# Row factors of the first norm moved onto results, with transposed input and three tiles side by side, and the convolutions of the up-projection emitted last

## Chip, core and metric

The kernel runs on one core of a Trainium2 chip. The metric is the device time of one execution in microseconds (us). The core has a matrix engine (TensorE, PE in the profile; PEld is its weight load), a vector engine (VectorE, DVE), a scalar engine for activations (ScalarE, ACT), GpSimd (POOL), and 16 DMA engines, which this kernel feeds from one queue, that of SyncE (SP).

## The reference

A hybrid decoder block for one sequence of 1024 positions and 1024 channels, in float32:

```
def rms_norm(x, w):
    y = x * rsqrt(mean(x * x, axis=-1) + EPS)
    return y * w

h = rms_norm(x, norm_mix_w)
proj = h @ w_in            # one product for all that follows:
q_nsa, kv_nsa, g_nsa, q_ret, k_ret, v_ret, g_ret, g_merge = split(proj)
y_a = nsa_attention(rope(q_nsa), kv_nsa, sigmoid(g_nsa)) @ w_nsa_branch
y_b = (group_norm(retention(q_ret, k_ret, v_ret)) * silu(g_ret)) @ w_ret_branch
x = x + (sigmoid(g_a) * y_a + sigmoid(g_b) * y_b) @ w_mix_out    # g_a, g_b from g_merge
h = rms_norm(x, norm_ffn_w)
u = causal_dwconv(h @ w_ffn_up)      # width 3, with a bias
x = x + (silu(u_gate) * u_val) @ w_ffn_down
return rms_norm(x, norm_final_w)
```

The factor 1/rms belongs to a row of x. It can be applied to the row before the product with w_in, or to the same row of the product's result.

## The kernel before

Rows are cut into NT = 8 tiles of 128 positions, channels into KT = 8 tiles of 128. Every float32 operand of a matrix product is split into a high part, a copy to the format fp32r on ACT, and a low part, the remainder, a subtraction on DVE (`split`, L174); `mm3` (L278) then does three products for each step: high by high, high by low, low by high.

First norm (L319 to L334): for each tile the rows are fetched into a buffer of the pool `big` (eight buffers), `normed` takes squares on ACT, the root, a few one-column steps on DVE and one scaling by rstd and gain, and `transposed_split` (L269) transposes the eight 128x128 blocks on PE and splits them into `hh` and `hl`, which hold h transposed. The weights of the first projection (`kvw`) are fetched in four pairs of channel tiles, two at t = 0 and two at t = 1, through two raw buffers (`wr`, pool `wraw`).

Projections: `proj` (L341) runs over the row tiles, 24 products of 512 columns each, and calls an evacuation for each tile. The first projection gives the keys and values of two branches (`evac_kv`), the next the third branch and the branch gates (`evac_kw`, 280 columns), then the queries (`evac_q`). The attention follows, with the products of the merge gates filled in between; their results are stored in DRAM transposed (`gate_d`). Then comes the retention (`evac_qk`, `values`, `evac_g`), and the merge: `gated` (L976) loads one merge gate of 128x1024 and takes its sigmoid; gates from the second eight use three buffers `gb`, which also serve sums of w_ffn_down (`t_sums`).

Up-projection (L1237 to L1299): 22 column tiles f, computed by a Strassen-like scheme with seven products of 12 matrix instructions each for one f. `first_weights` and `other_weights` fetch and split the weights of one f, with sums on DVE. The first five f have two of their seven products done earlier (`begun`). `up(f, w)` does the rest: each product is followed by a sum on DVE, and at the end two `conv` (one ACT step and two scalar_tensor_tensor steps on DVE each), a Silu, one multiplication and a store.

Tiles come from pools, and an instruction waits where its buffer is still in use. Where no order is written out by hand, each engine's instructions are ordered ahead of time, the one earlier in the program first where several are ready; each engine then runs its list in that order. In the stretches marked `manual_schedule` the order is that of the program (attention: that of a planner, `Plan`).

Of the kernel before, what the change touches and what calls it, by code (L numbers as in the profile page):

```python
# [10 lines left out]
F32 = mybir.dt.float32  # L11
# [7 lines left out]
P = 128  # L19
D = 1024  # L20
# [143 lines left out]
def hybrid_block(ctx: ExitStack, tc: tile.TileContext, a, c, out):  # L164
# [153 lines left out]

    with tc.tile_pool(name="n1", bufs=2, side="right") as n1:  # L319
        gain = n1.tile([P, D], F32, name="gain1", bufs=1)  # L320
        for t in range(NT):
            xt = big.tile([P, D], F32, name="big")
            n = 2 if t == 0 else 1
            for i in range(0, D, D // n):
                nc.sync.dma_start(xt[:, i:i + D // n], a["x"][0, t * P:(t + 1) * P, i:i + D // n])
            if t == 0:
                nc.sync.dma_start(gain, bcast_rows(a["norm_mix_w"][0], D))
                nc.sync.dma_start(ident, c["ident"])
            h = big.tile([P, D], F32, name="big")
            normed(n1, xt, gain, h, n)  # L330
            transposed_split(psA, h, hh, hl, t)
            if t < 2:
                kvw.more()
                kvw.more()  # L334
# [6 lines left out]
    def proj(w, n, evac, tag="mm", pool=None, other=iter(()), cuts=(0, KT), keep=0, pairs=False):  # L341


        last = NT - 2 if pairs else NT
        for t in range(NT):
            if t <= last:
                ps = [(pool or psA).tile([P, 512], F32, name=tag) for _ in range(2 if t == last else 1)]
                for k0, k1 in zip(range(0, KT, 2), range(2, KT + 1, 2)) if t == last else zip(cuts, cuts[1:]):
                    for i, x in enumerate(ps):
# [5 lines left out]
            evac(t, ps[0] if t <= last else ps[1])  # L355
# [38 lines left out]
    def v_store(b, t, ps):  # L394
        split(vhl[b][:, t, :, 0:DH], vhl[b][:, t, :, DH:], ps)
# [6 lines left out]
    def evac_kv(t, ps):  # L402
        nc.scalar.activation(kvc[:, t].rearrange("p a g d -> p (a g d)"), ps[:, 0:256], AF.Copy)
# [100 lines left out]
    def evac_q(t, ps):  # L504
        nc.scalar.activation(qsb[:, t].rearrange("p h d -> p (h d)"), ps, AF.Copy, scale=DH ** -0.5)
        rope16(qsb[:, t], t, H, np_)
# [296 lines left out]
    nc.sync.dma_start(rope, c["rope128"])  # L803
    dmask = rp.tile([P, RH, P], F32, name="dmask")
# [26 lines left out]
    for p in range(2):  # L831
# [48 lines left out]
        def values(t, ps):  # L880
            v = big.tile([P, 2, 2, DV], F32R, name="v", tag="big")
            split(v[:, 0], v[:, 1], ps.rearrange("p (h e) -> p h e", h=2))
# [121 lines left out]
    for ch in range(2):  # L1004
        nx = Weights(w_a, 0, 4, [(512, 512)]) if ch == 0 else Weights(w_b, 0, KT, [(0, 512)])
        for i in range(4):
# [7 lines left out]
            if (ch * 4 + i) % 2 == 0:  # L1014
                x, y = ([q[:, 0:512], q[:, 512:S]] for q in
                        (mp.tile([P, S], F32, name="tq", tag="gb", bufs=3) for _ in range(2)))
                t_sums(t_left.pop(0), x, y)
# [48 lines left out]
    c2p = ups.enter_context(tc.tile_pool(name="c2", bufs=10))  # L1066
# [144 lines left out]
    def other_weights(f):  # L1211
# [13 lines left out]
        hi, lo = (cpool.tile([P, 512], F32R, name=x, bufs=2) for x in ("a22h", "a22l"))  # L1225
# [11 lines left out]
    def up(f, w):  # L1237
# [51 lines left out]
    nx = other_weights(0)  # L1289
    for f in range(FT):  # L1290
# [8 lines left out]
        up(f, w)  # L1299
# [176 lines left out]
_LAYOUT = {"w_ffn_up": _up_layout}  # L1476
# [22 lines left out]
```

## Time and profile before

| | |
|---|---|
| median of 3 runs | 1786.49 us (1784.19 to 1790.05) |
| the profiled execution | 1786.91 us, of which the span of the core is 1785.1 us |
| busy share | PE 98%, DVE 67%, ACT 45%, POOL 7% |
| DMA | 188.32 MB, mean 105 GB/s over the span |

The profile shows one execution. The span runs from the first to the last instruction of the core. A group of instructions is given by line, engine, operation and tiles (out<-in). Products on PE overlap, so the length of one is not the step from one to the next.

### The profile page before, as it was taken

To read this page: it belongs to the slowest core of one execution; us is meant where nothing else is said; L and a number is where in the kernel's file an instruction comes from. 1 tells how busy PE (TensorE), PEld (TensorE's weight loads), DVE (VectorE), ACT (ScalarE), POOL (GpSimd) and SP (SyncE) were. 2 spreads that over 40 slices of the span, in tenths; PEclk is the share of its full clock that TensorE was granted. 3 is DMA by queue.
4 is the path that set the end of the run, shared out by engine and by line. 5 is a ranking of instruction groups with operands and counts; after the bars stand their busy time and mean duration, and the time that the engine had idled before them with its cause. 6 is when DMAs were issued, how large, how long until landed. Compare 5 with 4: busy or idle time off the path is not lost. (4 is left out here: it accounts for less than half of the span.)

```text
span 1785.1 us, 22560 instructions
## 1 busy us (share of the span) xinstructions
PE 1742.7 (98%) x8331; PEld 1430.9 (80%) x8331; DVE 1189.1 (67%) x2343; ACT 803.9 (45%) x1464; POOL 120.6 (7%) x72
## 2 busy tenths in 40 slices
PE   7999999999999999999999999889999999999998
PEld 6987888878788888888888878767888888878886
DVE  7445878787876554456455447877677677678666
ACT  6334666665654244136332215434444444353344
POOL 0000010020100000000000001201211211000000
PEclk9999999999999999999999999999999999999999
DMA  6121011020203101111485483323323323396353
GB/s 230 55 84 54 19 42 48 25 65 25 66 24 101 47 1 54 53 36 48 134 281 188 148 295 101 118 71 112 124 95 118 118 95 107 104 345 217 99 161 112
DMA packets 90155, 188.32 MB, mean 105 GB/s; under 512 B 8813, under 2 KB 18621, under 8 KB 90045
## 3 DMA queue, kind: packets, MB, share of 16 engines
q1 hardware_dynamic: 90044, 186.88, 32.0%
q8 instruction: 65, 1.06, 0.2%
q14 instruction: 46, 0.37, 0.1%
HBM read 147.00 MB, written 39.85 MB: 105 GB/s over the span
## 5 line engine op out<-in xcount | busy, mean ns | idle before, releaser
L283 PE MATMUL mm<-wh,hh 128*128 128x512 f32 (+1 forms) x576 | 224.1, 389 | 0.3 <-ACT hh L175 0.3
L283 PE MATMUL mm<-wh,hl 128*128 128x512 f32 (+1 forms) x576 | 220.0, 382 | 0.0
L283 PE MATMUL mm<-wl,hh 128*128 128x512 f32 (+1 forms) x576 | 219.8, 382 | 0.0
L209 ACT ACTIVATE wh<-wr 128x1024 fp32r<-128x1024 f32 (+1 forms) x72 | 74.6, 1037 | 154.9 <-PE mm L283 76.8
L175 ACT ACTIVATE wh<-wr 128x1024 fp32r<-128x1024 f32 (+1 forms) x87 | 88.3, 1020 | 102.5 <-PE f L283 49.7
L713 DVE TENSOR_TENSOR pl<-pt,ph 128x512 fp32r<-128x512 f32 (+1 forms) x148 | 100.7, 687 | 41.7 <-ACT ph L710 41.2
L283 PEld LDWEIGHTS mm<-wh,hh 128*128 128x128 f32 x576 | 108.8, 189 | 20.4 <-ACT wh L209 0.9
L283 PEld LDWEIGHTS mm<-wh,hl 128*128 128x128 f32 x576 | 108.7, 189 | 20.5 <-DVE hl L176 0.3
L710 ACT ACTIVATE ph<-pt 128x512 fp32r<-128x512 f32 (+1 forms) x148 | 87.7, 595 | 82.7 <-PE pt L706 74.4
L283 PEld LDWEIGHTS mm<-wl,hh 128*128 128x128 f32 x576 | 108.9, 189 | 19.5 <-DVE wl L215 0.5
L283 PE MATMUL f<-wh,sl 128*128 128x512 f32 x300 | 118.0, 395 | 0.8 <-DVE sl L176 0.8
L283 PE MATMUL f<-wh,sh 128*128 128x512 f32 x300 | 118.4, 395 | 0.0
L283 PE MATMUL f<-wl,sh 128*128 128x512 f32 x300 | 118.4, 395 | 0.0
L176 POOL TENSOR_TENSOR wl<-wr,wh 128x1024 fp32r<-128x1024 f32 x22 | 55.4, 2520 | 899.5 <-ACT wh L175 899.5
L283 PE MATMUL f<-bht,wh 128*128 128x512 f32 x264 | 105.2, 399 | 5.3 <-ACT wh L175 5.3
L283 PE MATMUL f<-bh,wh 128*128 128x512 f32 x264 | 104.2, 395 | 6.2 <-ACT c L1188 6.2
L283 PE MATMUL f<-bht,wl 128*128 128x512 f32 x264 | 105.4, 399 | 4.1 <-DVE wl L176 4.1
L215 DVE TENSOR_TENSOR wl<-wr,wh 128x1024 fp32r<-128x1024 f32 (+1 forms) x60 | 71.4, 1193 | 55.8 <-ACT wh L209 55.0
L772 PE MATMUL fill<-hh,wh 128*128 128x512 f32 x256 | 104.5, 408 | 3.1 <-ACT sg L784 2.1
L628 ACT ACTIVATE big<-big,st 128x640 f32<-128x640 f32 (+7 forms) x128 | 93.5, 731 | 28.0 <-DVE st L624 27.3
L283 PE MATMUL f<-blt,wh 128*128 128x512 f32 x264 | 105.1, 398 | 0.0
L283 PE MATMUL f<-bl,wh 128*128 128x512 f32 x264 | 103.6, 392 | 0.0
(286 smaller groups left out, 4135.1 us busy)
## 6 DMA issues: line engine op xcount, KB each, us to landing
wr<-in_w_ffn_up SPq DMA_DIRECT2D x44, 512.0 KB, 3.9
wr<-in_w_in SPq DMA_DIRECT2D x40, 512.0 KB, 3.7
tq<-in_w_ffn_down SPq DMA_DIRECT2D x44, 256.0 KB, 4.5
t<-tq SPq DMA_DIRECT2D x44, 256.0 KB, 2.8
v<-in_w_ffn_up SPq DMA_DIRECT2D x22, 512.0 KB, 4.3
act<-c SPq DMA_DIRECT2D x22, 512.0 KB, 2.8
wr<-t SPq DMA_DIRECT2D x20, 512.0 KB, 3.6
a<-act SPq DMA_DIRECT2D x33, 256.0 KB, 6.0
```

Of the source, the lines that this page charges most:

```text
L175: nc.scalar.activation(hi, src, AF.Copy)
L176: (engine or nc.vector).tensor_tensor(lo, src, f32(hi), OP.subtract)
L209: nc.scalar.activation(hi[:, :, :self.n], self.raw[len(self.hi)], AF.Copy)
L215: self.engine.tensor_tensor(lo[:, :, :self.n], self.raw[j], f32(self.hi[j][:, :, :self.n]), OP.subtract)
L283: nc.tensor.matmul(ps, stat(sp, kt), mov(mp, kt), start=(first and n == 0), stop=(last and n == 3 * nk - 1), skip_group_check=more)
L628: nc.scalar.activation(probs[b][h], probs[b][h], AF.Exp, scale=-1.0, bias=stat["nm", b][:, h:h + 1], accum_out=stat["w", b][:, h:h + 1])
L710: nc.scalar.activation(bx["h"][:rows], bx["pt"][:rows], AF.Copy)
L713: nc.vector.tensor_tensor(bx["l"][:rows], bx["pt"][:rows], f32(bx["h"][:rows]), OP.subtract)
L772: nc.tensor.matmul(fx["ps"], w.at(sp, kt, i * P, P), hT[mp][:, kt, half * 512:half * 512 + 512], start=(n == 0), stop=(n == 3 * KT - 1))
```

## The change

**First norm.** `x` is also given transposed (`x_t`), and the gain as a column per channel tile. For each row tile the transposed block is fetched, multiplied by the gain on DVE and split straight into `hh` and `hl`, without the factor of the row. The rows of x are fetched too, for the mean square; the factors are kept in `rs` and, for the merge, stored in DRAM (`rs_d`). The weight pairs are asked for around the first tile, and the first three tiles of the first projection run side by side (`lead=3`): each weight pair serves the three before the next.

**Row factors on results.** Each evacuation of a projection multiplies by its row's factor: keys and the compressed branch in their ACT copy, values in `scaled_split`, branch gates in a DVE step, queries with the scale folded into `rs_q`, retention queries and keys through the rope table, its gate in the Silu. The merge gates, stored transposed, are multiplied by a broadcast of all factors (`rb`) on DVE before the sigmoid. The buffers `gb` fall from three to two.

**Up-projection.** `finish(f, ...)` holds both convolutions, the Silu, the product and the store; `up(f, ...)` calls it for f - 1 at its very end, and calls `other_weights(f + 1)` after its third product. `c2` falls from ten to nine buffers, `c4` rises from six to seven, and `a22h`, `a22l` fall from two to one each.

```
     with tc.tile_pool(name="n1", bufs=2, side="right") as n1:
-        gain = n1.tile([P, D], F32, name="gain1", bufs=1)
+        gain = n1.tile([P, KT], F32, name="gain1", bufs=1)
+        nc.sync.dma_start(gain, a["norm_mix_w"])
         for t in range(NT):
-            xt = big.tile([P, D], F32, name="big")
+            xt = big.tile([P, KT, P], F32, name="big")
+            src = a["x_t"].rearrange("(k p) s -> p k s", p=P)[:, :, t * P:(t + 1) * P]
             n = 2 if t == 0 else 1
-            for i in range(0, D, D // n):
-                nc.sync.dma_start(xt[:, i:i + D // n], a["x"][0, t * P:(t + 1) * P, i:i + D // n])
+            for k in range(0, KT, KT // n):
+                ks = slice(k, k + KT // n)
+                nc.sync.dma_start(xt[:, ks], src[:, ks])
+                if t == 0 and k == 0:
+                    kvw.fetch()
+                nc.vector.tensor_mul(xt[:, ks], xt[:, ks],
+                                     gain[:, ks, None].to_broadcast([P, KT // n, P]))
+                split(hh[:, ks, t * P:(t + 1) * P], hl[:, ks, t * P:(t + 1) * P], xt[:, ks])
             if t == 0:
-                nc.sync.dma_start(gain, bcast_rows(a["norm_mix_w"][0], D))
+                kvw.high()
+                kvw.low()
+                for _ in range(3):
+                    kvw.more()
                 nc.sync.dma_start(ident, c["ident"])
-            h = big.tile([P, D], F32, name="big")
-            normed(n1, xt, gain, h, n)
-            transposed_split(psA, h, hh, hl, t)
-            if t < 2:
-                kvw.more()
-                kvw.more()
+            x = big.tile([P, D], F32, name="big")
+            nc.sync.dma_start(x, a["x"][0, t * P:(t + 1) * P, :])
+            *_, v = mean_square(n1, [x], [x])
+            nc.vector.tensor_copy(rs[:, t:t + 1], rstd_of(n1, v))
...
+    nc.vector.tensor_scalar(rs_q, rs, DH ** -0.5, None, op0=OP.mult)
+    rs_d = dram.tile([NT, P], F32, name="rs_d")
+    nc.sync.dma_start(rs_d.rearrange("t p -> p t"), rs)
+
+    def scaled_split(hi, lo, src, t):
+        r = rs[:, t:t + 1]
+        nc.scalar.activation(hi, src, AF.Copy, scale=r)
+        nc.vector.scalar_tensor_tensor(lo, src, r, f32(hi), op0=OP.mult, op1=OP.subtract)
...
-        last = NT - 2 if pairs else NT
+        groups = {0: lead, **({NT - 2: 2} if pairs else {})}
+        ready = []
         for t in range(NT):
...
+            if not ready:
+                ready = [(pool or psA).tile([P, 512], F32, name=tag) for _ in range(groups.get(t, 1))]
+                at = range(0, KT + 1, 2) if len(ready) > 1 else cuts
+                for k0, k1 in zip(at, at[1:]):
+                    for i, x in enumerate(ready):
...
-        nc.scalar.activation(ks, ps, AF.Copy)
+        nc.scalar.activation(ks, ps, AF.Copy, scale=rs[:, t:t + 1])
...
-        split(vhl[b][:, t, :, 0:DH], vhl[b][:, t, :, DH:], ps)
+        scaled_split(vhl[b][:, t, :, 0:DH], vhl[b][:, t, :, DH:], ps, t)
...
-    proj(kvw, 512, evac_kv)
+    proj(kvw, 512, evac_kv, lead=3)
...
-        nc.vector.tensor_copy(gates[:, t].rearrange("p h b -> p (h b)"), ps[:, 256:280])
+        nc.vector.tensor_scalar(gates[:, t].rearrange("p h b -> p (h b)"), ps[:, 256:280], rs[:, t:t + 1], None,
+                                op0=OP.mult)
...
+    for i in range(2):
+        nc.vector.tensor_mul(rope[:, i], rope[:, i], rs[:, :, None].to_broadcast([P, NT, DK // 2]))
...
-            nc.scalar.activation(sg, ps, AF.Silu)
+            nc.scalar.activation(sg, ps, AF.Silu, scale=rs[:, t:t + 1])
...
+    rb = mp.tile([P, S], F32, name="rb")
+    nc.sync.dma_start(rb, bcast_rows(rs_d, S))
+
     def gated(j):
-        m = mp.tile([P, S], F32, name=f"ma{j % KT}" if j < KT else "gb", bufs=1 if j < KT else 3)
+        m = mp.tile([P, S], F32, name=f"ma{j % KT}" if j < KT else "gb", bufs=1 if j < KT else 2)
         nc.sync.dma_start(m, gate_d[j])
+        nc.vector.tensor_mul(m, m, rb)
         nc.scalar.activation(m, m, AF.Sigmoid)
         return m
...
-    c2p = ups.enter_context(tc.tile_pool(name="c2", bufs=10))
+    c2p = ups.enter_context(tc.tile_pool(name="c2", bufs=9))
...
-    cpool = ups.enter_context(tc.tile_pool(name="cp", bufs=6, reuse_waits="tile"))
+    cpool = ups.enter_context(tc.tile_pool(name="cp", bufs=1, reuse_waits="tile"))
...
-        return cpool.tile([P, 2, 512], F32, name="c4")
+        return cpool.tile([P, 2, 512], F32, name="c4", bufs=7)
...
-        hi, lo = (cpool.tile([P, 512], F32R, name=x, bufs=2) for x in ("a22h", "a22l"))
+        hi, lo = (cpool.tile([P, 512], F32R, name=x) for x in ("a22h", "a22l"))
...
-    def up(f, w):
+    def finish(f, cg, cv):
+        yg = conv(cg.rearrange("p a b -> p (a b)"), f)
+        nc.scalar.activation(yg, yg, AF.Silu)
+        yv = conv(cv.rearrange("p a b -> p (a b)"), FT + f)
+        nc.vector.tensor_mul(yg, yg, yv)
+        nc.sync.dma_start(act_d[f], yg.rearrange("p (a b) -> p a b", b=512))
+
+    def up(f, w, before):
+
         x, p1 = begun.pop(f, None) or start_up(fw[f])
...
         nc.vector.tensor_add(cv[:, 1], z, u3)
+        nx = other_weights(f + 1) if f + 1 < FT else None
         if f >= LEAD:
...
-        yg = conv(cg.rearrange("p a b -> p (a b)"), f)
-        nc.scalar.activation(yg, yg, AF.Silu)
-        yv = conv(cv.rearrange("p a b -> p (a b)"), FT + f)
-        nc.vector.tensor_mul(yg, yg, yv)
-        yg = yg.rearrange("p (a b) -> p a b", b=512)
-        nc.sync.dma_start(act_d[f], yg)
+        if before:
+            finish(*before)
+        return (f, cg, cv), nx
...
     for f in range(FT):
-        w, nx = nx, None
-        if f + 1 < FT:
-            if f + 1 >= LEAD:
-                fw[f + 1] = first_weights(f + 1)
-            nx = other_weights(f + 1)
+        if f + 1 < FT and f + 1 >= LEAD:
+            fw[f + 1] = first_weights(f + 1)
...
-        up(f, w)
+        left, nx = up(f, nx, left)
+    finish(*left)
```

## Rows read from the trace of the kernel before

**Rows 1.** The page's first part: busy time, share of span, instructions of each engine.
```profile
PE 1742.7 (98%) x8331; PEld 1430.9 (80%) x8331; DVE 1189.1 (67%) x2343; ACT 803.9 (45%) x1464; POOL 120.6 (7%) x72
```
**Rows 2.** Windows: length, busy of PE, PEld, DVE, ACT, POOL; PEclk, DMA share, GB/s.
```profile
0.00:66.80 66.80, 57.68 (x271) 45.61 (x271) 38.32 (x117) 34.19 (x85) 2.86 (x9) 1.00 0.48 158
600.00:700.00 100.00, 99.94 (x534) 85.72 (x533) 55.23 (x134) 47.17 (x89) 0.00 (x0) 1.00 0.15 43
930.00:1010.00 80.00, 80.00 (x355) 66.24 (x354) 42.17 (x40) 20.90 (x20) 0.00 (x0) 1.00 0.48 164
1100.00:1147.00 47.00, 40.75 (x184) 32.60 (x183) 44.02 (x64) 27.05 (x51) 14.68 (x6) 0.96 0.32 104
1147.00:1245.00 98.00, 88.60 (x362) 69.49 (x361) 71.09 (x82) 37.40 (x40) 11.22 (x7) 0.97 0.27 91
1245.00:1560.00 315.00, 315.00 (x1368) 256.37 (x1367) 229.93 (x263) 134.14 (x147) 55.91 (x30) 1.00 0.33 109
1560.00:1785.10 225.10, 217.24 (x935) 175.65 (x933) 157.19 (x203) 96.67 (x132) 0.00 (x0) 0.99 0.56 187
2.00:11.00 9.00, 1.97 (x8) 1.57 (x8) 2.65 (x8) 3.37 (x10) 0.00 (x0) 1.00 0.93 306
```
**Rows 3.** Waits of PE: line, waited for; us in total, times, longest.
```profile
PE tp L275 <- DVE big L267: 8.8, 1, 8.8
PE f L283 <- ACT c L1188: 6.2, 4, 3.2
PE f L283 <- ACT wh L175: 5.3, 3, 2.2
PE f L283 <- DVE wl L176: 4.1, 4, 1.2
```
**Rows 4.** Timeline of the first stage: start, length, engine, line, operation, idle before.
```profile
0.74 0.87 SPq L325 DMA_DIRECT2D big<-in_x  x2
3.39 0.63 ACT L256 ACTIVATE big<-big 128x512 f32<-128x512 f32 x1 [1.16 <-DMA big<-in_x]
8.78 1.97 PE L275 MATMUL tp<-ident,big 128*128 128x128 f32 x8 [8.78 <-DVE big L267]
11.09 0.79 PE L283 MATMUL mm<-wh,hh 128*128 128x512 f32 x1 [0.34 <-ACT hh L175]
...
16.05 0.63 PE L283 MATMUL mm<-wl,hh 128*128 128x512 f32 x1
...
66.80 0.37 PE L283 MATMUL mm<-wh,hh 128*128 128x280 f32 x1
```
**Rows 5.** Timeline of PE: transposes between products, and 18 steps of products.
```profile
37.40 0.39 PE L283 MATMUL mm<-wl,hh 128*128 128x512 f32 x1
37.76 1.06 PE L275 MATMUL tp<-ident,big 128*128 128x128 f32 x8
38.58 0.47 PE L283 MATMUL mm<-wh,hl 128*128 128x512 f32 x1
...
45.19 0.39 PE L283 MATMUL mm<-wh,hl 128*128 128x512 f32 x1
...
49.29 0.39 PE L283 MATMUL mm<-wh,hl 128*128 128x512 f32 x1
```
**Rows 6.** DMA, 35 to 40 us: queue, packets, MB, share of 16 engines.
```profile
q1 hardware_dynamic: 1550, 1.54, 93.1%
```
**Rows 7.** Timeline around one stall of PE in the up-projection.
```profile
1184.93 2.47 DVE L1233 SCALAR_TENSOR_TENSOR c<-c,cw,c 128x1023 f32<-128x1023 f32 x2
...
1189.70 0.69 DVE L1218 TENSOR_TENSOR c<-c,wr 128x512 f32<-128x512 f32 x1
1190.42 1.06 ACT L175 ACTIVATE wh<-c 128x1024 fp32r<-128x1024 f32 x1 [0.68 <-DVE c L1218]
1191.53 0.50 PE L283 MATMUL f<-bht,wh 128*128 128x512 f32 x1 [2.24 <-ACT wh L175]
1192.04 1.22 DVE L176 TENSOR_TENSOR wl<-c,wh 128x1024 fp32r<-128x1024 f32 x1
```

More of the change, by code (lines that the diff above doesn't have):

```diff
@@ L317, in hybrid_block @@
     kvw = Weights(w_in, 0, KT, [(C_KV, 512)], late=True)
+    rs = const.tile([P, NT], F32, name="rs")
     with tc.tile_pool(name="n1", bufs=2, side="right") as n1:
-        gain = n1.tile([P, D], F32, name="gain1", bufs=1)
+        gain = n1.tile([P, KT], F32, name="gain1", bufs=1)
+        nc.sync.dma_start(gain, a["norm_mix_w"])
         for t in range(NT):
-            xt = big.tile([P, D], F32, name="big")
+            xt = big.tile([P, KT, P], F32, name="big")
+            src = a["x_t"].rearrange("(k p) s -> p k s", p=P)[:, :, t * P:(t + 1) * P]
             n = 2 if t == 0 else 1
-            for i in range(0, D, D // n):
-                nc.sync.dma_start(xt[:, i:i + D // n], a["x"][0, t * P:(t + 1) * P, i:i + D // n])
+            for k in range(0, KT, KT // n):
[6 more added lines that the diff above has]
+                split(hh[:, ks, t * P:(t + 1) * P], hl[:, ks, t * P:(t + 1) * P], xt[:, ks])
             if t == 0:
-                nc.sync.dma_start(gain, bcast_rows(a["norm_mix_w"][0], D))
+                kvw.high()
+                kvw.low()
+                for _ in range(3):
+                    kvw.more()
                 nc.sync.dma_start(ident, c["ident"])
-            h = big.tile([P, D], F32, name="big")
-            normed(n1, xt, gain, h, n)
-            transposed_split(psA, h, hh, hl, t)
-            if t < 2:
-                kvw.more()
-                kvw.more()
+            x = big.tile([P, D], F32, name="big")
+            nc.sync.dma_start(x, a["x"][0, t * P:(t + 1) * P, :])
+            *_, v = mean_square(n1, [x], [x])
+            nc.vector.tensor_copy(rs[:, t:t + 1], rstd_of(n1, v))
+    rs_q = const.tile([P, NT], F32, name="rs_q")
+    nc.vector.tensor_scalar(rs_q, rs, DH ** -0.5, None, op0=OP.mult)
[5 more added lines that the diff above has]
+        nc.vector.scalar_tensor_tensor(lo, src, r, f32(hi), op0=OP.mult, op1=OP.subtract)
     def h_stat(t):
@@ L339, in hybrid_block, with proj @@
     later = []
-    def proj(w, n, evac, tag="mm", pool=None, other=iter(()), cuts=(0, KT), keep=0, pairs=False):
-        last = NT - 2 if pairs else NT
+    def proj(w, n, evac, tag="mm", pool=None, other=iter(()), cuts=(0, KT), keep=0, pairs=False, lead=1):
+        groups = {0: lead, **({NT - 2: 2} if pairs else {})}
+        ready = []
         for t in range(NT):
[L346 to L349, printed above, removed]
+            if not ready:
[3 more added lines that the diff above has]
+                    for i, x in enumerate(ready):
                         mm3(x[:, :n], lambda part, kt: h_stat(t + i)(part, k0 + kt),
@@ L354, in proj @@
                 later.pop(0)()
-            evac(t, ps[0] if t <= last else ps[1])
+            evac(t, ready.pop(0))
     r16 = np_.tile([P, 2, NT, ROT], F32, name="r16")
@@ L402, in evac_kv @@
     def evac_kv(t, ps):
-        nc.scalar.activation(kvc[:, t].rearrange("p a g d -> p (a g d)"), ps[:, 0:256], AF.Copy)
+        nc.scalar.activation(kvc[:, t].rearrange("p a g d -> p (a g d)"), ps[:, 0:256], AF.Copy,
+                             scale=rs[:, t:t + 1])
         k_store("s", t, g64(ps[:, 256:384]))
@@ L504, in evac_q @@
     def evac_q(t, ps):
-        nc.scalar.activation(qsb[:, t].rearrange("p h d -> p (h d)"), ps, AF.Copy, scale=DH ** -0.5)
+        nc.scalar.activation(qsb[:, t].rearrange("p h d -> p (h d)"), ps, AF.Copy,
+                             scale=rs_q[:, t:t + 1])
         rope16(qsb[:, t], t, H, np_)
@@ L881, in values @@
             v = big.tile([P, 2, 2, DV], F32R, name="v", tag="big")
-            split(v[:, 0], v[:, 1], ps.rearrange("p (h e) -> p h e", h=2))
+            scaled_split(v[:, 0], v[:, 1], ps.rearrange("p (h e) -> p h e", h=2), t)
             ch[t]["v"] = (v[:, 0], v[:, 1])
@@ L1015, in hybrid_block @@
                 x, y = ([q[:, 0:512], q[:, 512:S]] for q in
-                        (mp.tile([P, S], F32, name="tq", tag="gb", bufs=3) for _ in range(2)))
+                        (mp.tile([P, S], F32, name="tq", tag="gb", bufs=2) for _ in range(2)))
                 t_sums(t_left.pop(0), x, y)
@@ L1289, in hybrid_block @@
     nx = other_weights(0)
+    left = None
     for f in range(FT):
-        w, nx = nx, None
-        if f + 1 < FT:
-            if f + 1 >= LEAD:
-                fw[f + 1] = first_weights(f + 1)
-            nx = other_weights(f + 1)
+        if f + 1 < FT and f + 1 >= LEAD:
+            fw[f + 1] = first_weights(f + 1)
         if f == FT - 1:
@@ L1473, in _up_layout @@
     return np.ascontiguousarray(w.transpose(4, 2, 3, 0, 1, 5)).reshape(FT, P, 4 * 512)
-_LAYOUT = {"w_ffn_up": _up_layout}
+_LAYOUT = {"w_ffn_up": _up_layout, "norm_mix_w": lambda w: w[0].reshape(KT, P).T}
 _OUT = ((1, S, D), "float32")
@@ L1492 @@
     a = {k: given(k, _LAYOUT.get(k, lambda v: v)(v)) for k, v in inputs.items()}
+    a["x_t"] = given("x_t", inputs["x"][0].T)
     c = {k: given("c_" + k, v) for k, v in _constants().items()}
```

## The prediction

> **What bounds the kernel now.** I read the page's busy times first: PE is busy in 98% of the span, DVE in 67%, ACT in 45% [rows 1]. So the span is PE's work plus the gaps in it. I then cut the span by stage [rows 2] and asked in each how much PE stood still. Up to 66.8 us (first norm and first projection) 9.1 us are missing; from 1100 to 1147 (last rows of the residual and first products of the up-projection) 6.3; from 1147 to 1245 (up-projection, f = 0 to 4) 9.4; from 1245 to 1560 (f = 5 to 21) nothing; in the last stretch 7.9, which the diff leaves alone. Elsewhere only PE's own instructions can be saved. The waits of PE name the same places [rows 3]: 8.8 us for the first normalised rows, 6.2 for a copy at L1188, 5.3 and 4.1 for the split weights wh and wl, which all lie between 1147 and 1245. The change touches the first and the last two of these; the L1188 wait is in the leading products, whose code does not change.
>
> **Part 1, the first norm.** Removed: 64 PE transposes at L275. Eight of them between two products cost 1.18 us less the usual step [rows 5]. That step is (49.29 - 45.19) / 18 = 0.228 us a product, so eight cost 0.95 and 64 cost 7.6 us. Also gone is the chain in front of the first product: half a row tile needs 2.65 us from issue to use, then come squares, root, scaling, transposes and split, and the first product starts at 11.09 [rows 4].
>
> New chain: the gain is now 4 KB and goes first, so the transposed half is issued near 1.2 and lands near 3.8; multiplication on DVE and the ACT copy are 128x512 steps of 0.6 to 0.7 each (a DVE step of that size took 0.69 [rows 7]), so hh stands at 5.2. The first weight pair is the third issue, at about 1.7; I give it 4 us, to 5.7, and 1.06 for its ACT copy: first product at 6.8.
>
> The stage before ends at 66.80, where the 280-wide products begin [rows 4]. What stays is 8 tiles of 24 products, 192 x 0.228 = 43.7 us; 16 key transposes, 1.9 us at the same price; and about twelve products at half pace in the beginning (the one at 16.05 is 0.63 long [rows 4], a normal one 0.39 [rows 5], so each costs about 0.2 more; the granted clock of that stretch reads 1.00 all the same [rows 2]), 2.4 us. If nothing starves, the stage ends at 6.8 + 43.7 + 1.9 + 2.4 = 54.8: 12 us gained.
>
> It will starve, because x is now fetched twice, 4 MB more. The queue's price: in a stretch filled by 1 KB packets, 93.1% of 16 engines x 5 us over 1550 packets is 48 ns a packet [rows 6]. A tile of x or a weight pair (512 KB, 32 KB an engine) takes 1.5 us. A transposed tile has 1024 packets of 512 B, 64 an engine: no row shows such packets in number, so 1.5 us (by bytes) to 3.1 (as long as a 1 KB packet). PE takes a tile in 24 x 0.228 = 5.5 us, so 3.0 to 4.6 us a tile keep up in the long run. The trouble is the beginning. The pool big has eight buffers, now all filled by DMA, so four tiles in both forms can be issued at once, while the third and fourth weight pair need a raw buffer back (two exist), after the first pair's split: near 8 us. If they queue behind all of that, 12 to 18.4 us of tiles and 3 of weights go first, and the third pair lands between 18.6 and 25. After it come 2.3 us of conversion (1.06 + 1.22 [rows 7]), 156 products (35.5 us) and the turns: end between 58.3 and 64.7, a gain of 8.5 to 2.1. Side by side, three tiles give PE up to 36 products with two pairs, so it is not idle all the while. I take the third pair near 20, end 59.7, gain 7; bounds 2 and 12.
>
> The Trainium skill ("DMA: Bandwidth & Descriptors", section "Why small descriptors are slow") gives each packet about 3 fixed cycles beside one per 32 bytes. An estimate from that page is 19 cycles for 512 B against 35 for 1 KB, so 26 ns a packet and 1.7 us a transposed tile. By it the third pair would land at about 19.4 and the gain be 7.7; no run here shows it yet.
>
> DVE and ACT do not grow: the scaling by rstd and gain (128x1024) becomes a multiplication by the gain of that size, the split reads SBUF instead of PSUM, squares and roots stay. Each evacuation takes the row factor inside an instruction that was there (an ACT scale; a scalar_tensor_tensor in place of a subtraction of the same size; for the gates a tensor_scalar in place of a copy): priced at nothing, since PE has no gap beside them, and DVE is busy 57% in the first stage and 55% in the projections of the retention [rows 2]. An evacuation now waits for its row's statistics; the row's DMA stands right behind its transposed tile, so I see that wait only for tiles 0 to 2, whose products end last of all. The factors go to DRAM once, in 4-byte pieces, with 1000 us until they are read.
>
> **Part 2, merge gates.** Sixteen multiplications of 128x1024 on DVE, 1.22 us each as the split of that size [rows 7]: 19.5 us, 1.2 per gate, of which one is used every 10 us in the stretch where DVE is busy 42 of 80 us and PE has no gap [rows 2]. Hidden. The pool gb falls from three buffers to two: one gate lives for one 10.9 us round (48 products), the next is loaded in the other, a load and two steps of about 8 us. Cost 0; bound 3 us if the w_ffn_down sums, which share the buffers, hold the SP queue before a gate. c2 falls from ten to nine buffers: x1[1][1] waits for row 0 to end, with half a round to spare. Cost 0, bound 2.
>
> **Part 3, the up-projection.** Read the stall at 1191.53 [rows 7]: DVE runs both pairs of convolution steps (L1233 2.47 us for its pair, then L1234) from 1184.93 to 1189.70; only then L1218, whose result ACT copies at 1190.42; PE gets wh at 1191.53 after 2.24 us of waiting, and wl after a further wait. The same happens for three f, with a smaller one for a fourth: 5.3 + 4.1 = 9.4 us [rows 3]. The granted clock in this stretch is 0.97 [rows 2]: 0.03 / 0.5 x 98 = 5.9 us at the lower level, where half the work (2.9 us) is lost; so the gaps cost more than their length. The whole is worth up to 12.3 us.
>
> The change emits the convolutions of f-1 behind all of f, and the preparation of f+1 behind f's third product. Where instructions are ordered by program order, DVE then finds sums and splits first. Preparation: sum of the z product 0.69, two subtractions 1.4, ACT 1.06, wl 1.22, and hops: 4.7 us. For f = 0 to 4 two products of 12 follow (24 x 0.228 = 5.5 us), so it fits with 0.8 to spare. Is there DVE for it? One f is nine 128x512 steps (6.2), two wl and one product of 128x1024 (3.7), four convolution steps (4.9): 14.8 us against 60 x 0.228 = 13.7 of PE. Over four f that is 4.5 us too much, and the delay of one f puts 6.2 us of it off to f >= 5, where PE needs 84 x 0.228 = 19.2 us. It just fits, so I take 9 of 12.3 back; bounds 0 (the order does not change) and 12.3. The a22 pair falls to one buffer: its split waits for the a22 product of f, and is needed 10 us later; nothing. c4 has seven buffers, and cg, cv of two f, two results and one sum are seven: no spare, no wait.
>
> **Sum.** 1785.1 - 7 - 9 = 1769.1, and 1.8 us lie around the span: 1771. The runs' median is 0.4 us under the profiled execution, so the same number stands for it.
>
> **Rivals.**
> (a) Only the up-projection gains: the tiles do stand ahead of the weights, at 3.1 us each. For it: the queue was already filled to 0.93 between 2 and 11 us [rows 2]. 1786.9 - 2 - 9 = 1776.
> (b) Only the start gains: the window of 5.5 us is missed, because the DMA of f+1 or an ACT step comes late; the waits on wh and wl stay. 1786.9 - 7 = 1780.
> (c) Neither: starved start, same stalls. 1786.9 - 2 = 1785.
> (d) Slower: the steady stage f = 5 to 21, which has no gap now, gets one in every f. The splits for f+1 begin only after the third product of f; until f+1's first use four products remain (48 x 0.228 = 10.9 us). With 4.7 us needed, 6.2 us may come in between on DVE; the convolutions of f-1 with their product (4.9 + 1.2) are just that. If DVE takes them first and a POOL split slows it, 1.2 us a time are missing: 17 x 1.2 = 20. 1786.9 - 7 + 20 = 1800. Against it: they are last in order, and DVE is idle for a quarter of that stage [rows 2].
>
> **How the numbers follow.** Both gains 0.60, (a) 0.12, (b) 0.12, (c) 0.08, (d) 0.08. A measurement of this kernel tells about 0.3% (5.4 us) from no change, so below 1781 is faster: both gains, (a) and half of (b), 0.78; same 0.14; slower 0.08. The likeliest case alone spans 1762 (12 and 12.3 gained) to 1777. The range takes in (a) and (b) and reaches to the edge of (c): 1762 to 1784, leaving out (d) and about half of (c).
>
> **What would show it.** Right: no L275; first product near 7 us and 280-wide products from about 59; wh and wl waits of PE between 1130 and 1230 mostly gone, with the granted clock there at 1.00; DVE's L1218-type step ahead of the convolutions; f >= 5 still without gaps. Wrong: PE waiting for the third weight pair past 25 us, for an evacuation's row factor, or for wh in every f.

## The result and the profile after

The changed kernel takes 1776.81 us (median of 5 runs, 1774.99 to 1780.61) against 1786.49 (1783.12 to 1790.05): ratio 0.9940, 95% interval 0.9924 to 0.9957, or 9.7 us gained. The prediction said 1771 and a gain of 16, with a range of 1762 to 1784. The profiled execution is the longest of the five: 1780.61 us, span 1778.8.

First the page's busy times and windows of the changed kernel, to be laid beside [rows 1] and [rows 2] (same columns).

```profile
PE 1734.5 (98%) x8267; PEld 1423.9 (80%) x8267; DVE 1268.7 (71%) x2363; ACT 802.2 (45%) x1455; POOL 125.0 (7%) x72
```
```profile
15.00:20.00 5.00, 3.14 (x10) 1.92 (x10) 3.69 (x4) 3.04 (x4) 0.00 (x0) 0.82 1.08 360
...
40.00:45.00 5.00, 4.22 (x20) 3.03 (x18) 4.53 (x24) 3.28 (x10) 1.28 (x4) 1.00 0.22 59
...
900.00:920.00 20.00, 20.00 (x102) 16.69 (x101) 16.98 (x20) 7.72 (x10) 0.00 (x0) 1.00 0.76 264
920.00:940.00 20.00, 16.25 (x69) 12.82 (x68) 11.36 (x14) 5.80 (x8) 0.00 (x0) 0.91 0.69 235
...
1147.00:1245.00 98.00, 94.32 (x405) 75.28 (x404) 82.25 (x88) 40.60 (x45) 14.15 (x9) 1.00 0.29 99
1245.00:1550.00 305.00, 305.00 (x1331) 249.48 (x1330) 272.47 (x254) 123.42 (x143) 57.56 (x30) 1.00 0.33 109
```

DVE's work grew by 80 us; the multiplications of gates explain 20. In the up-projection PE's missing time in 1147 to 1245 fell from 9.4 to 3.7 us, at a clock of 1.00. New gaps stand at 15 to 20, at 40 to 45 and at 920 to 940 us. The waits of PE name them, over the whole span (columns as in [rows 3]):

```profile
PE mm L283 <- ACT wh L209: 8.0, 2, 7.0
PE f L283 <- ACT c L1219: 6.2, 4, 3.3
PE mm L283 <- DVE ma L1043: 3.8, 2, 3.2
PE f L283 <- DVE sl L176: 2.9, 1, 2.9
PE f L283 <- DVE c L1285: 2.4, 2, 1.6
...
PE mm L283 <- DVE vs L354: 1.4, 1, 1.4
PE f L283 <- DVE wl L176: 1.0, 2, 0.8
```

Of the first row 7.0 us are the time before the first product (8.8 before, then for a transpose). L1188 of before is L1219 now, unchanged. The waits for wh and wl in the up-projection, 5.3 and 4.1, are 0 and 1.0. The wait for L1043 (the product times the gate) in the merge is new, and that for the sums `sl`, at the change to the down-projection, grew from 0.8 to 2.9.

Where the time went is seen best from a few products whose start every trace has. Each column is the time from one mark to the next; the marks are the first 280-wide product, the last product that reads `oaT` (first branch), the last that reads `orT` (second branch), the first and the last with the `t` tiles of `bh` (up-projection) and the last that reads `sh` (down-projection). The table is worked out from the rows of each trace.

| kernel | to 280-wide | to last oaT | to last orT | to first bh t | to last bh t | to last sh |
|---|---|---|---|---|---|---|
| before | 66.8 | 855.8 | 89.2 | 133.9 | 413.6 | 218.2 |
| changed | 63.2 | 858.9 | 94.5 | 131.2 | 401.7 | 221.1 |
| changed, second profile (after2) | 61.2 | 857.6 | 93.5 | 130.5 | 401.8 | 221.1 |
| e1_up | 67.1 | 855.8 | 89.2 | 131.9 | 403.7 | 221.7 |
| e2_norm | 61.2 | 855.9 | 92.5 | 131.2 | 414.2 | 219.1 |
| e3_gb2 | 66.8 | 855.8 | 89.6 | 133.1 | 416.8 | 218.2 |
| e4_nomul | 60.6 | 856.8 | 90.8 | 130.3 | 401.8 | 221.1 |
| g3_sums | 61.8 | 857.0 | 92.0 | 137.3 | 401.8 | 221.1 |
| m1_odd | 61.2 | 857.7 | 90.8 | 133.8 | 401.7 | 223.8 |
| s1_order | 62.4 | 856.7 | 92.5 | 132.0 | 401.7 | 221.1 |
| f4_last | 60.9 | 855.9 | 89.3 | 131.2 | 401.7 | 219.7 |
| f5_dve | 61.0 | 857.1 | 93.2 | 132.0 | 398.9 | 222.6 |
| c1_three | 59.6 | 857.4 | 89.0 | 131.9 | 398.9 | 219.7 |
| c2_four | 62.4 | 858.5 | 93.7 | 131.5 | 398.9 | 219.5 |

So the changed kernel gains 3.6 at the start and 11.9 in the up-projection, loses 5.3 in the merge and 2.9 in the down-projection, gains 2.7 between, and loses 3.1 in the attention: 6.9, less 0.6 behind the last product, is the 6.3 us between the spans.

**The start.** Timeline of SP, PE and DVE in the first 20 us:

```profile
3.76 0.43 SPq L343 DMA_DIRECT2D big<-in_x  x1
9.20 0.38 SPq L202 DMA_DIRECT2D wr<-in_w_in  x1
9.62 0.47 SPq L330 DMA_DIRECT2D big<-in_x_t  x1
...
6.98 0.80 PE L283 MATMUL mm<-wh,hh 128*128 128x512 f32 x1 [6.98 <-ACT wh L209]
...
18.94 0.80 PE L283 MATMUL mm<-wh,hh 128*128 128x512 f32 x1 [0.33 <-ACT hh L175]
...
15.44 1.22 DVE L333 TENSOR_TENSOR big<-big,gain 128x1024 f32<-128x1024 f32 x1
```

The first product is at 6.98 us. SP's queue then stands still from 4.2 to 9.2: the third weight pair needs a raw buffer, and transposed tile 1 is behind it in the queue. Tile 1 is multiplied at 15.44 and used from 18.94 on; products of tile 0 alone fill the time until then, most of them at half pace, with gaps where the next weight pair is late. The three tiles did not run side by side: tile 0 ran ahead alone.

**The convolutions.** Timeline of POOL and DVE for one f of the steady stage; L1249 is L1218 of the kernel before:

```profile
1295.01 0.69 DVE L1249 TENSOR_TENSOR c<-c,wr 128x512 f32<-128x512 f32 x1
...
1299.95 1.30 POOL L176 TENSOR_TENSOR a22l<-v,a22h 128x512 fp32r<-128x512 f32 x1 [14.64 <-ACT a22h L175]
1302.04 2.55 POOL L176 TENSOR_TENSOR wl<-wr,wh 128x1024 fp32r<-128x1024 f32 x1 [0.79 <-ACT wh L175]
...
1300.00 5.67 DVE L1264 SCALAR_TENSOR_TENSOR c<-c,cw,c 128x1023 f32<-128x1023 f32 x2
...
1306.20 2.46 DVE L1265 SCALAR_TENSOR_TENSOR c<-c,cw,c 128x1022 f32<-128x1022 f32 x2
```

The sums now come first, as intended, and L1264's pair falls on GpSimd's two splits. It takes 5.67 us, where L1265's pair of the same size, with GpSimd idle, takes 2.46.

**The merge.** Timeline of DVE behind the first branch, and the product of PE that waits for it:

```profile
922.09 0.69 DVE L1023 TENSOR_TENSOR tq<-tq 128x512 f32<-128x512 f32 x1 [1.26 <-DMA tq<-in_w_ffn_down]
...
924.38 0.69 DVE L1024 TENSOR_TENSOR tq<-tq 128x512 f32<-128x512 f32 x1 [1.00 <-DMA tq<-in_w_ffn_down]
...
927.58 1.22 DVE L1043 TENSOR_TENSOR ma<-mm,ma 128x1024 f32<-128x1024 f32 x1
...
928.85 0.73 PE L283 MATMUL mm<-orT,wh 128*128 128x512 f32 x2 [3.19 <-DVE ma L1043]
```

The last product of the first branch ended before 923 us, but its multiplication is behind a set of w_ffn_down sums in DVE's list, and these wait for their data. PE stops for 3.2 us, and then runs at a granted clock of 0.70 from 928 to 932 and 0.88 from 932 to 936. So the loss has two parts: from 920 to 940 us the clock is 0.91 as a mean, 0.09 / 0.5 x 20 = 3.6 us at the lower level, half of it lost; with the wait that is 5.0 of the 5.3 us.

The wait follows the fetch of that fourth set, which needs buffers `gb`. SP's first issue of it, in the kernel before, the changed kernel and c1_three:

```profile
911.76 0.78 SPq L989 DMA_DIRECT2D tq<-in_w_ffn_down  x1
```
```profile
918.47 0.36 SPq L1020 DMA_DIRECT2D tq<-in_w_ffn_down  x1
```
```profile
910.13 0.36 SPq L1038 DMA_DIRECT2D tq<-in_w_ffn_down  x1
```

Against the last `oaT` product (922.6, 922.0 and 917.0 us) that is 10.8, 3.6 and 6.8 us ahead.

### The profile page after: what moved, and what is told of

It is laid out like the page before. It is cut to its first block, busy times and chain, and to the rows that moved or that the text cites. A ratio compares the mean times of both kernels' runs of the same rounds, so it can differ in the third digit from the quotient of the medians.

```text
span 1778.8 us, 22477 instructions
## 1 busy us (share of the span) xinstructions
PE 1734.5 (98%) x8267; PEld 1423.9 (80%) x8267; DVE 1268.7 (71%) x2363; ACT 802.2 (45%) x1455; POOL 125.0 (7%) x72
## 4 chain that ended last, share of the span: by engine, by line
PE 61%; DVE 4%; DMA 4%; issue 3%; ACT 1%; SPq 1%; POOL 0%; DVEq 0%; ACTq 0%; POOLq 0%
PE f L283 32%; PE mm L283 20%; PE fill L797 3%; DMA tq<-in_w_ffn_down 1%; PE po L853 1%; PE pv L743 1%; DMA wr<-in_w_ffn_up 1%; PE pt L731 1%; PE sc L635 1%; DVE c L1264 1%; DMA t<-tq 1%; PE pst L853 1%; DMA wr<-in_w_mix_out 1%; DVE wl L176 0%; DVE c L1265 0%
## 5 line engine op out<-in xcount | busy, mean ns | idle before, releaser
L1264 DVE SCALAR_TENSOR_TENSOR c<-c,cw,c 128x1023 f32<-128x1023 f32 x44 | 106.8, 2462 | 0.4 <-ACT c L1263 0.4
L283 PE MATMUL f<-bh,wl 128*128 128x512 f32 x264 | 103.9, 394 | 0.0
```

Of the source, the lines that this page charges most:

```text
L283: nc.tensor.matmul(ps, stat(sp, kt), mov(mp, kt), start=(first and n == 0), stop=(last and n == 3 * nk - 1), skip_group_check=more)
L1264: nc.vector.scalar_tensor_tensor(y[:, 1:], src[:, :S - 1], cw[:, 1, f:f + 1], y[:, 1:], op0=OP.mult, op1=OP.add)
```

## The experiments

**e1_up and e2_norm: each part alone.** The same edit, put into the kernel before (e1) and taken out of the changed kernel (e2):

```
+    left = None
     for f in range(FT):
...
+        left, nx = up(f, nx, left)
+    finish(*left)
```

> The kernel before with the third part of the change alone: finish() for f - 1 behind up(f), other_weights(f + 1) behind the third product, seven c4 and one buffer each for a22h and a22l; first norm, gates and buffers gb and c2 as before. Theory 1 (the parts are independent, and the up-projection carries the gain): its stage from the first product with bh t2 to the last falls from 407.7 us to about 396, as in the changed kernel, and the run is 11 to 12 us under the one before less 2 to 3 us for the sums sl behind two convolutions at the change to the down-projection, so 8 to 10 us, about 0.995. Rival (the up-projection gains only because the rows of the stage ahead of it end in another order after the change): under 4 us, 0.998 or more.

> The changed kernel with the third part undone: up(f), other_weights, c4 and a22 as in the kernel before; first norm, row factors and gates stay as changed. Theory 1: start 3.6 us gained, merge about 5 us lost, mix about 2 us gained: between 1 us lost and 2 us gained in all, 1.000. Rival (the row factors gain by themselves, as the prediction had it, 7 us): 0.996.

Measured: e1_up 1780.8 us, ratio 0.9946 (0.9927 to 0.9964); e2_norm 1783.97, 0.9974 (0.9960 to 0.9989). PE's waits, first of e1_up (its L1254 is L1285 of the changed kernel), then of e2_norm:

```profile
PE f L283 <- DVE sl L176: 2.8, 1, 2.8
...
PE f L283 <- DVE c L1254: 2.1, 2, 1.5
```
```profile
PE f L283 <- ACT wh L175: 5.7, 3, 2.4
PE f L283 <- DVE wl L176: 4.2, 4, 1.2
PE mm L283 <- DVE ma L1043: 2.5, 2, 2.1
```

Theory 1 holds. The third part alone takes 10.0 us from the up-projection and brings the wait for `sl` with it. The other 1.9 of the 11.9 us are not the order of the work: over 1000 products of the stretch without gaps the step from one to the next is 230.6 ns in the kernel before, e1_up and e3_gb2, and 229.5 ns in every profile with the new first norm, e2_norm too. Why is not shown. The first two alone leave the waits for wh and wl, bring the wait in the merge, and start 5.6 us earlier; their ratio lies between what theory 1 and its rival gave, as the start gained 2 us more than in the first profile of the changed kernel. The two ratios multiply to 0.992, with 0.994 inside the uncertainty.

**e3_gb2, e4_nomul, g3_sums and m1_odd: the merge.** The edit of g3 is abridged.

```
e3:  before with   name ... "gb", bufs=... 3 -> 2   and   tag="gb", bufs=3 -> 2
e4:  -        nc.vector.tensor_mul(m, m, rb)
g3:  -            if (ch * 4 + i) % 2 == 0:        +            if ch * 4 + i in (0, 2, 4):
     -                if j in (2, 4, 6):  (ma{j-2}, ma{j-1})
     +                if j in (1, 3, 5, 7):  (ma{j-1}, ma{j})
m1:  -            if (ch * 4 + i) % 2 == 0:        +            if (ch * 4 + i) % 2 == 1:
```

> The kernel before with one edit: the pool tag gb has two buffers instead of three. Theory 2 (the 3.8 us that PE waits for the last merge product of the first branch come from the buffers: the sums of w_ffn_down stand in DVE's list ahead of that multiplication and their fetch waits for a buffer): PE waits 2 to 4 us at the change from the first to the second branch, and the run is 3 to 5 us longer, 1.002. Rival (the eight multiplications by the row factors fill DVE there, buffers or not): no such wait, and the same time to 0.1%.

> The changed kernel without the multiplication of the merge gates by rb (so their row factors are left out of the computation); two buffers gb stay. Theory 2 (buffers): the wait of 3 to 4 us for the multiplication by the gates stays, and the time is that of the changed kernel to 0.1%. Rival (multiplications on DVE): the wait goes, orT ends about 4 us earlier, and the ratio to the kernel before is 0.992 instead of 0.994.

> The changed kernel with the fourth set of w_ffn_down sums taken out of the first branch of the merge (there they stand behind gates 0, 2 and 4 only) and given to the second, where sets now stand behind products 1, 3, 5 and 7. Theory 2b (the last multiplication by a gate waits in DVE's list behind the fourth set, whose fetch waits for one of two buffers gb, and the multiplications by rb make that later; neither alone is enough): the wait of PE for L1043 goes, orT ends 4 us earlier against the end of the first branch, and the ratio to the kernel before is about 0.9915. Rival (DVE is simply too full there with eight multiplications more): the wait only moves, 0.994.

> The changed kernel with one edit: in the first branch of the merge the sums of w_ffn_down stand behind products 1, 3, 5 and 7 instead of 0, 2, 4 and 6, so that the last multiplication by a gate no longer has a set of sums between it and the one before. Theory 2c (place in DVE's list): the wait of PE for L1043 at 920 us falls under 1 us, with it the clock stays at 1.00 there, and from the last oaT to the last orT product it takes 90 us instead of 92 to 94.5: ratio 2 to 4 us under that of the changed kernel. Rival (DVE is too full between 905 and 925 us whatever the order): PE waits as long for orT or for L1043.

Measured: e3_gb2 1787.84 us, 0.9983 (0.9970 to 0.9995); e4_nomul 1772.22, 0.9896 (0.9879 to 0.9914); g3_sums 1780.58, 0.9947 (0.9926 to 0.9969); m1_odd 1775.89, 0.9933 (0.9919 to 0.9948). The 20 us ahead of the gap, as windows, of the kernel before, of e3_gb2 and of e4_nomul:

```profile
900.00:920.00 20.00, 20.00 (x101) 16.51 (x100) 12.48 (x17) 7.27 (x10) 0.00 (x0) 1.00 0.90 310
```
```profile
900.00:920.00 20.00, 20.00 (x100) 16.53 (x99) 11.50 (x16) 8.39 (x13) 0.00 (x0) 1.00 0.89 298
```
```profile
900.00:920.00 20.00, 20.00 (x102) 16.41 (x100) 12.96 (x18) 9.11 (x13) 0.00 (x0) 1.00 0.81 283
```

PE's waits of e4_nomul in the merge (its L1042 is L1043) and of g3_sums in the stage after it:

```profile
PE mm L283 <- DVE ma L1042: 1.9, 1, 1.9
```
```profile
PE f L1120 <- DVE h L1145: 3.3, 2, 2.3
```

Two buffers alone make a wait of 0.8 us and no loss: theory 2 falls in its plain form. Without the multiplications DVE is busy 13.0 of the 20 us instead of 17.0, and the wait is 1.9 us instead of 3.8 in all. The ratio falls below those of the changed kernel, 0.9940 and, in a second timing, 0.9936 (0.9922 to 0.9950), and the intervals do not overlap. So the sixteen multiplications have a price, but where it is paid is not shown: of the 4.3 us between the spans of e4_nomul and after2 2.7 lie in the merge, and its 90.8 us there lie among the 89.0 to 94.5 that profiles with the changed kernel's merge take. To take the fourth set of sums away (g3_sums) leaves 0.2 us of the wait for L1043 at the change of branches and puts 1.1 us of waiting for `orT` in its place; the stage still takes 92.0 us, and 3.3 us come back as a wait for `h` in the residual (137.3 us to the first `bh t`): the rival's "only moves". To set the sums behind odd products (m1_odd) leaves 2.1 us of waiting, 1.7 of them at the change of branches where theory 2c gave under 1; the clock from 920 to 940 stays at 1.00 and the stage takes 90.8 us, near its 90, but the ratio is that of the changed kernel. In this one profile the stretch to the first `bh t` takes 3.3 us more than in after2 and that to the last `sh` 2.7 more, at a granted clock of 0.97 and 0.98 instead of 0.99 and 1.00.

What stays open: f4_last and c1_three have the merge's code as it is in the changed kernel and take 89.3 and 89.0 us there, where the five others take 92.5 to 94.5 (f4_last's profile is of the shortest of its six runs). In these two the fourth set's first fetch is issued 6.6 and 6.8 us ahead of the last `oaT` product, PE waits 0.5 and 0.2 us at the change of branches, and the clock stays at 1.00; in the five it is issued 3.6 to 6.0 us ahead, PE waits 2.0 to 3.2 us, and the clock of the 20 us behind is 0.91. In f4_last DVE waited 0.9 us for the set's data, in after2 2.7 us. Why the issue comes earlier in some executions of the same code is not shown. Here is c1_three, to be laid beside the row 920 to 940 of the changed kernel:

```profile
920.00:940.00 20.00, 20.00 (x88) 16.59 (x89) 10.25 (x11) 4.13 (x4) 0.00 (x0) 1.00 0.55 189
```

**s1_order: the order of the first fetches.** Tiles 1 and 2 of `x_t` are fetched and split behind the second weight pair; the two other pairs and the rows of x follow.

```
+        kvw.more()
+        for t in (1, 2):
+            xts[t] = big.tile([P, KT, P], F32, name="big")
+            fetch_t1(t, 1, 0)
+            split_t1(t, 1, 0)
+        kvw.more()
+        kvw.more()
```

> The changed kernel with another order of the first fetches: the transposed tiles 1 and 2 are asked for behind the second weight pair and ahead of the third and fourth, and every row tile of x behind all of these. Theory 3 (the start is short of the second and third tile, whose fetch stands in SP's queue behind the third weight pair, which waits for a raw buffer until 9.2 us): the 7 us wait of PE behind tile 0 goes, the 280-wide products begin at 54 to 57 us instead of 60.6 to 63.2, and the ratio to the kernel before is about 0.991 instead of 0.994. Rival (the queue's 340 GB/s are the bound, and the order only exchanges waits): the 280-wide products begin at 60 us or later, 0.994.

Measured: 1774.55 us, 0.9911 (0.9890 to 0.9931), which overlaps the changed kernel's interval. (The 7 us in the expectation are the time before the first product, misread.) Windows of s1_order, then of c1_three, which has the same start:

```profile
15.00:20.00 5.00, 5.00 (x24) 4.12 (x23) 3.83 (x10) 3.58 (x7) 0.00 (x0) 1.00 0.99 326
...
35.00:40.00 5.00, 3.66 (x17) 2.69 (x15) 5.00 (x26) 3.85 (x10) 1.92 (x3) 1.00 0.95 307
40.00:45.00 5.00, 3.81 (x12) 2.89 (x13) 3.53 (x23) 3.12 (x12) 0.87 (x2) 0.63 0.38 8
45.00:50.00 5.00, 5.00 (x18) 3.91 (x17) 0.55 (x2) 0.67 (x3) 0.00 (x0) 0.69 0.75 35
```
```profile
35.00:40.00 5.00, 3.75 (x17) 2.79 (x15) 5.00 (x25) 4.04 (x10) 1.46 (x2) 1.00 0.95 308
40.00:45.00 5.00, 3.72 (x19) 2.87 (x20) 4.14 (x25) 3.78 (x13) 0.96 (x3) 1.00 0.31 11
45.00:50.00 5.00, 5.00 (x25) 4.08 (x24) 0.72 (x5) 1.26 (x4) 0.00 (x0) 1.00 0.77 36
```

Theory 3 is right about the gap at 15 to 20 us, which is gone, and wrong about the end. PE now reaches the last tiles early and stands 2.5 us in all at 38 to 42, where DVE is busy without a break: low parts of the last tile, root steps of the row factors and the splits of keys and values all stand in its list. The rival's time, 60 us or later, came true in this profile, but its cause did not: it named the queue; it is DVE. With the clock held the first projection ends at 59.57 (c1_three), with the clock down behind the same gap at 62.40.

**f4_last and f5_dve: the end of the up-projection, and the splits of GpSimd.**

```
f4:  -        nx = other_weights(f + 1) if f + 1 < FT else None
     +        nx = other_weights(f + 1) if f + 1 < FT else finish(*before)
     -        if before:            +        if before and f + 1 < FT:
f5:  -        p = parts2(raw_up(f), nc.gpsimd)
     +        p = parts2(raw_up(f), nc.gpsimd if f < LEAD else nc.vector)
     -        split(hi, lo, v[:, 1], nc.gpsimd)      +        split(hi, lo, v[:, 1], nc.vector)
```

> The changed kernel with one edit: for the last f, 21, finish() for f = 20 comes behind the third product, in the place where other_weights would stand, instead of at the end. Theory 4 (PE waits 2.9 us for a sum sl at the change to the down-projection because the convolutions of f = 20 and 21 then stand in DVE's list one behind the other): the wait falls to the 0.8 us of the kernel before, 2 us gained. Rival (the 5.7 us of convolutions ahead of the last sums of f = 21 delay the first act tiles as much): the wait stays at 2 to 3 us, no gain.

> The changed kernel with the low parts of the first weights (f = 5 to 21) and of a22 on DVE instead of GpSimd. Theory 5 (the first convolution step takes 2.4 us each on average instead of 1.28 because GpSimd's split runs at the same time, and a DVE step with both operands in SBUF waits for it): L1264 is back at 1.28 us each, some 50 us of DVE time go and about 36 come for the moved splits, DVE's busy time falls from 1269 to about 1253 us, and the run is the same to 0.1%, as PE had no gap there. Rival (the step is long for another reason, traffic of the queue or its operands): L1264 stays near 2.4 us, DVE has more than the 19.3 us of one f, and PE gets a gap in every f: 10 us or more slower.

Measured: f4_last 1772.28 us, 0.9907 (0.9884 to 0.9929); f5_dve 1773.31, 0.9915 (0.9893 to 0.9937). The groups of the convolution steps by line (busy us, mean ns), of the changed kernel and of f5_dve, and PE's one wait of f4_last in 1530 to 1600 us:

```profile
L1264 DVE SCALAR_TENSOR_TENSOR c<-c,cw,c 128x1023 f32<-128x1023 f32 x44 | 106.8, 2462 | 0.4 <-ACT c L1263 0.4
```
```profile
L1264 DVE SCALAR_TENSOR_TENSOR c<-c,cw,c 128x1023 f32<-128x1023 f32 x44 | 54.7, 1279 | 0.4 <-ACT c L1263 0.4
```
```profile
PE f L283 <- ACT p L1429: 0.9, 1, 0.9
```

Both theories hold in their mechanism. The wait for `sl` is gone (1.4 us less from the last `bh t` to the last `sh` product; a wait of 0.9 for `p` is left). L1264 is back at 1279 ns, DVE's busy time at 1243 us, though it has 39 splits more. "The same to 0.1%" was not quite right: f5_dve's up-projection is 2.9 us shorter in all three profiles that have the edit, since PE did wait for DVE in f = 0 to 4; 1.6 of them come back at the change to the down-projection, and with f4's edit they do not.

**after2, c1_three and c2_four: the changed kernel again, and edits together.** c1 is s1, f4 and f5; c2 adds m1.

> The changed kernel itself, unaltered, beside the next three. Theory 6 (what its first profile shows at 450 to 500 us, a granted clock of 0.93, and its clock of 0.82 to 0.84 from 15 to 25 us belong to that one execution): the first projection ends between 60.6 and 62 us as in the experiments with the same start, the attention takes the 855.7 us from the first projection's end to the last oaT product of the kernel before to within 1, and the ratio is between 0.992 and 0.995. Rival (the start that runs ahead is given back in the attention by its planned order): the last oaT product comes less than 1 us earlier than in the kernel before.

> The changed kernel with three edits together: the order of the first fetches (s1), finish() of f = 20 behind the third product of f = 21 (f4), and the low parts of first weights and a22 on DVE (f5). If their effects add: 0.994 less 0.001 for the order, 0.0012 for the last sums and nothing for the split: 0.991 to 0.992. Rival: with f5 the transition is already eased and the two do not add: 0.993.

> The three edits of c1 and the sums behind odd products (m1). By theory 2c 2 to 4 us under c1: 0.989 to 0.990. By its rival the same as c1.

Measured on one chip: after2 1776.41 us, 0.9936 (0.9922 to 0.9950); c1_three 1766.67, 0.9885 (0.9867 to 0.9904); c2_four 1770.5, 0.9904 (0.9888 to 0.9921). The window 450 to 500 us, first of the changed kernel's first profile, then of after2:

```profile
450.00:500.00 50.00, 47.66 (x239) 38.60 (x238) 38.49 (x100) 29.91 (x66) 7.29 (x3) 0.93 0.21 64
```
```profile
450.00:500.00 50.00, 47.66 (x251) 38.88 (x251) 37.59 (x98) 29.77 (x64) 7.31 (x3) 0.97 0.20 63
```

The start ends at 61.19, and the last `oaT` product comes 3.8 us earlier than before: the rival of theory 6 falls. Theory 6 falls in part too: the attention takes 1.8 us longer than in the kernel before, not less than 1. PE's busy time in 450 to 500 us is the same in both profiles, and the clock of 0.97 is worth 0.03 / 0.5 x 50 = 3 us at the lower level, half of it lost. c1_three is the best kernel here, 9.7 us under after2 by the medians, more than the separate edits promised; of the 9.1 us between the two profiles' spans 4.3 are the up-projection and the down-projection, 1.6 the start, and 4.4 the merge, whose 89.0 us no edit of c1 explains, less 1.4 in the stretch behind it. The 4.4 are luck as far as is known. c2_four gives no support to m1's edit: its merge takes 93.7 us.

## Why the prediction was right or wrong

**Faster: right,** and for the part that carried it. The size, 16 us, was too large by 6, though the two gains forecast came nearly whole (3.6 + 11.9 = 15.5 us in the first profile). What was wrong are terms put at nothing or not in the sum: the merge, the down-projection and the attention. The range held because it was wide enough for the rivals, not because these losses were foreseen.

**Up-projection, gain 9: right in mechanism, too small.** It brought 10.0 us alone and 11.9 in the changed kernel. DVE's order is the predicted one, the waits for wh and wl fell from 9.4 to 1.0 with 2.4 of a new one for L1285, the clock rose to 1.00. That the 12.3 us of the upper bound were nearly reached is luck for 1.9 of them, the shorter step of products. The single a22 pair, the c4 and the c2 buffers, priced at nothing, show in no wait of PE, and the wait for the copy in the leading products is the same 6.2 us.

**Rival (d), its premise:** GpSimd's splits did slow the convolutions, by 52 us in all (106.8 against 54.5), but no gap came in f = 5 to 21. The quarter of DVE's time that the prediction named against it took it up: DVE was busy 73% there, and is 89% now.

**The change to the down-projection, not in the sum.** "Convolutions of f-1 behind all of f" leaves two sets for the end of the last f, one behind the other in DVE's list, ahead of the first `sl`: 2.1 us more waiting, 2.9 us in the stage (e2_norm, without the third part, loses 0.9 there too). The step that failed is that the order was worked out for the middle of the loop alone; the change moved something past the loop's end as well.

**Start, gain 7: 3.6 to 6.2 in eight profiles.** First product at 6.8: 6.98. The step that failed is the order of the queue. The prediction had tiles issued ahead of the weight pairs, which starve; in fact the third pair, itself waiting for a buffer, stood ahead of tiles 1 and 2, so that the tiles starved. With that order changed the stage ends at 59.6 us (c1_three) instead of 61.2 (after2). The price of a transposed tile was bounded by 1.5 and 3.1 us. The queue in 20 to 30 us, by packets:

```profile
DMA packets 3984, 3.38 MB, mean 338 GB/s; under 512 B 98, under 2 KB 3595, under 8 KB 3984
```

Both forms of a tile, 1.05 MB, take 1.05 / 0.338 = 3.1 us. In the trace the 3497 packets of 512 B of this stretch took 31 ns each and the 389 of 4 KB 178 ns, and packets overlap; shared out in this proportion a transposed tile takes near 1.8 us and a row tile 1.3. The Trainium skill ("DMA: Bandwidth & Descriptors", section "Why small descriptors are slow") led to an estimate of 1.7; the trace agrees to 0.1 us.

**"DVE and ACT do not grow" and "PE has no gap beside them": failed** at 40 to 45 us. With the transposes gone PE arrives earlier at the last tiles, and DVE is then the one that is late (4.53 of 5 us, and 5.00 in s1_order). PE waits 1.4 us there for the evacuation `vs` (L354) of tile 2, whose row factor had been ready since 27 us: it is not the factor that is late; the steps of the evacuation stand behind others in the lists of ACT and DVE. The 57% were a mean over a stage.

**Merge gates, cost 0, bound 3: failed.** The stage takes 3.3 to 5.3 us longer in five of the seven profiles with this code, and no longer in two. "Hidden" rested on the 42 of 80 us behind 930 [rows 2]; the first eight gates lie ahead of that window, where DVE went from 12.5 to 17.0 of 20 us. The wait is the one that was bounded, sums that share the buffers `gb`. The bound left out the clock behind the wait, 1.8 us. How full DVE is does not set the wait by itself: in the last 20 us ahead of the last `oaT` product DVE is busy 15.6 us in the changed kernel and 18.3 in c1_three, where the wait is 0.2 us. What goes with it is how late the fourth set is fetched; what part the third buffer and the multiplications each have in that is not shown.

**Not foreseen:** the 2.7 us gained between merge and up-projection go with the granted clock of that stretch, which is 0.97 in the kernel before, e3_gb2 and m1_odd (133.1 to 133.9 us) and 0.99 in the profiles with 130.3 to 132.0, e1_up among them, so they are not shown to be the change's. The clock in 450 to 500 us differs between executions too, but it is 1.00 in all three profiles without the new first norm and below it, 0.93 to 0.97, in eight of the eleven with it; whether the change brings this is not shown.

## What to carry to other kernels

Price added work on an engine by its busiest stretch beside the critical path, not by the mean of a stage, and a buffer taken away by how much later the next fetch into it is issued. When work is put off by one turn of a loop, ask what stands at the loop's end, where two turns meet. The DMA queue of this kernel was held up for 5 us by one issue that waited for a buffer (4.2 to 9.2 us), so put what needs no buffer ahead of it; and work that is moved in time can fall on another engine's work.

## What the runs showed of the hardware

**A DVE step with both tensors in SBUF did not run beside a GpSimd split.** The pair at 1300.00 took 3.21 us longer than the 2.46 of L1265's pair, against 3.85 us of GpSimd's work in that time; without GpSimd (f5_dve) a step took 1279 ns instead of 2462. The Trainium skill ("SBUF — State Buffer", section "SBUF: two separate sides") says that a DVE step with two inputs in SBUF and a GpSimd instruction that reads SBUF need the same pair of ports, and that whoever comes second is blocked for the whole instruction; the trace agrees.

**The same short gap costs more in some executions than in others.** The gap at 38 to 42 us is followed by a granted clock of 0.63 and 0.69 in s1_order, of 0.60 and 0.71 in c2_four, and of 1.00 in c1_three, all with the same start. In s1_order and c1_three PE resumes at 41.9 and 42.0 us, and the first projection ends 2.8 us apart, more than the gap itself.
